# TensorE's order in the out product and the first MLP products, by a scheduler and written out

## The chip, the cores and the metric

The kernel runs on one core of a Trainium2 chip. The time is device microseconds (us) of one execution. Before the change three timed runs gave 2256.86, 2263.51 and 2263.76 us, median 2263.51.

## The reference

One layer of a decoder trunk, 1024 tokens of width 1024, float32: token mixing (dilated attention and an RWKV-7 branch, merged by gates), then an MLP. The stage at hand lies between the two halves:

```python
mix_out = merged @ w_out[l]
x = (x + gt1 * rms_norm(mix_out, norm_mix_post[l])).astype(x.dtype)

h = rms_norm(x, norm_ffn_pre[l]) * (1.0 + sc2) + sh2
f = jnp.square(jax.nn.relu(h @ w_ff1[l])) @ w_ff2[l]
```

## The kernel before

Each float32 operand is split into a high part (a cast on ScalarE) and a low part (a subtraction, mostly on VectorE), and each product is three matmuls: high by high, high by low, low by high. `split` (L64, L65) does this.

The out product (`out_product`) works by row blocks of 128 tokens, 0 to 7. `product(q, i, half)` is 24 matmuls (8 slices of the inner dimension by 3) for row block i and 512 of the 1024 columns. All first halves come first; each is copied from PSUM to `mx` (L993). A *row step* R then makes the second halves of one or two row blocks: two blocks use the two halves of one PSUM tile `d` (two buffers), each half a bank of its own. It copies them to `my` (L1014), sums squares on ScalarE (L1016), makes the factor of the first norm (`rr`, by `mean_rsqrt`, L1117 to L1127), multiplies (`junk`, L1025), adds to `x` on GpSimd and VectorE (L1027), sums squares again (L1030), makes the second factor and scales `x` on ScalarE (L1033).

A *transpose step* T takes the scaled `x` of a step: per row block two sets of four transposes into a PSUM tile `s` (two buffers, L1044). One set is read by two VectorE instructions (L1053, L1054), the other by four of ScalarE (L1049). Row blocks 0 to 3 give `hh0`, `hl0`, high and low part of the first 512 tokens of `h`; row blocks 4 to 7 give `h1`, and each of them a part of `T2`, one operand of the MLP's products (L1059 to L1061 and a split).

`ff1_head` makes products of the first 512 tokens by the left column halves of `w_ff1`, in pairs H of two groups, H0, H2, H4 and H6. A pair is four *quarters* of 12 matmuls, two in each half of one tile `d`: group 0 and group 1 with the upper half of the inner dimension (each copied to `u` on ScalarE, L1090), then both with the lower (each read by `ft`, L1100). Its weights come by DMA (`w_t`, three buffers) and are split to `w_h`, `w_l` (eight buffers each, one pair's worth).

`ff1` then makes the rest of the first MLP product by a seven-product scheme into tiles `m` (L1108, as the quarters). It begins with the operands `T3`, `T1`, `T4` and `B22`, made from `h1` and `hh0`, `hl0` of all 512 columns (L1146 to L1156 and splits; 20 instructions of VectorE over 1024 columns), and with sums and splits of weights (`t`, L1173 to L1176, `op`).

The order of each engine's instructions comes from a scheduler, which moves independent matmuls into each other's gaps; dependencies are by whole tile, so a write into one half of `d` waits for a read of the other half that stands ahead of it in the program. Instructions given to `keep_in_program_order` hold their order on their engine. The lines of the order in the program:

```python
todo.append((group, residual(group)))
if len(todo) > 1:
    transposed(*todo.pop(0))
```

so a transpose step is written one row step late, with H0 ahead of T7 and H2 to H6 behind it; where they stand in the end the scheduler decides.

Of the kernel before, what the change touches and what calls it, by code (L numbers as in the profile page):

```python
# [21 lines left out]
KT = D // 128  # L22
# [5 lines left out]
C_GATE = C_QKV + 3328  # L28
DFF = 4096
NH, NU, NF, NOP, NHW = 8, 4, 3, 12, 8  # L30
OGR = ((0, 1), (2, 3), (4,), (5,), (6,), (7,))
OPV = 0
OQ = 0
NBD, NFT, NLT, NW, NGT, NRK = 5, 6, 3, 4, 2, 4
# [15 lines left out]
class Block:  # L50
    def __init__(self, tc, ins, out, dbg=None):
        self.tc, self.nc, self.I, self.out, self.dbg = tc, tc.nc, ins, out, dbg or {}

    def dump(self, name, ap):
        if name in self.dbg:
            self.nc.sync.dma_start(self.dbg[name], ap)
# [908 lines left out]
    def out_product(self, cst, big, w1, ut, ft, psD, psS, xS):  # L965
        nc, tc = self.nc, self.tc
        hs = (slice(0, 512), slice(512, 1024))
        tc.keep_in_program_order(nc.scalar.preload_act_table_set("natural_log_exp_and_others"))
        with ExitStack() as es:
# [9 lines left out]
            def product(p, i, half):  # L979
                hi, lo = wos[half]  # L980
                mh, ml = self.mh[i // 4], self.ml_[i // 4]
                tl = slice(128 * (i % 4), 128 * (i % 4) + 128)
                for k in range(KT):
                    for n, (a, b) in enumerate(((mh, hi), (mh, lo), (ml, hi))):
                        nc.tensor.matmul(p, a[:, k, tl], b[:, k, :], start=k == 0 and n == 0,
                                         stop=k == KT - 1 and n == 2)

            for i in range(NT):
                if i % 2 == 0:
                    p = psD.tile([128, S], F32, name="d")  # L990
                q = p[:, hs[i % 2]]
                product(q, i, 0)
                nc.vector.tensor_copy(mx[:, i, :], q)  # L993
                junk = t2.tile([128, D], BF16, name="junk2", bufs=1)[:, 0:512]
                nc.scalar.activation(junk, mx[:, i, :], AF.Square, accum_out=ss[:, 0, i:i + 1])
            hhs, hls = [], []

            def residual(group):
# [8 lines left out]
                for n, i in enumerate(group):  # L1007
                    x = t2.tile([128, D], F32, name="x", bufs=4)
                    nc.sync.dma_start(x, self.w("x")[128 * i:128 * i + 128, :])
                    xs.append(x)  # L1010
                    q = p[:, hs[n]]
                    product(q, i, 1)
                    with tc.high_priority():
                        nc.vector.tensor_copy(my[:, n, :], q)  # L1014
                        junk = t2.tile([128, D], BF16, name="junk2", bufs=1)[:, 0:512]
                        nc.scalar.activation(junk, q if OQ else my[:, n, :], AF.Square, accum_out=ss[:, 1, i:i + 1])  # L1016
# [19 lines left out]
            def transposed(group, xs):  # L1036


                for n, i in enumerate(group):
                    x, tl = xs[n], slice(128 * (i % 4), 128 * (i % 4) + 128)  # L1040
                    for b in range(2):
                        pt = psS.tile([128, 4, 128], F32, name="s")
                        for k in range(4):
                            nc.tensor.transpose(pt[:, k, :], x[:, 512 * b + 128 * k:512 * b + 128 * k + 128],  # L1044
                                                self.ident)
                        ht = t2.tile([128, 4, 128], F32, name="ht") if i < 4 else self.h1[:, 4 * b:4 * b + 4, tl]
                        if b:
                            for k in range(4):
                                nc.scalar.activation(ht[:, k, :], pt[:, k, :], AF.Identity,  # L1049
                                                     scale=sc[:, 4 + k:5 + k], bias=sh[:, 4 + k:5 + k])  # L1050
                        else:
                            bc = lambda c: c[:, 0:4, None].to_broadcast([128, 4, 128])
                            nc.vector.tensor_tensor(ht, pt, bc(sc), OP.mult)  # L1053
                            nc.vector.tensor_tensor(ht, ht, bc(sh), OP.add)  # L1054
                        if i < 4:
                            self.split(ht, self.hh0[:, 4 * b:4 * b + 4, tl], self.hl0[:, 4 * b:4 * b + 4, tl])
                    if i >= 4:
                        t = t2.tile([128, 4, 128], F32, name="ht")
                        nc.vector.tensor_tensor(t, self.h1[:, 0:4, tl], self.hh0[:, 0:4, tl].bitcast(F32), OP.subtract)  # L1059
                        nc.vector.tensor_tensor(t, t, self.hl0[:, 0:4, tl].bitcast(F32), OP.subtract)  # L1060
                        nc.vector.tensor_tensor(t, self.h1[:, 4:8, tl], t, OP.subtract)  # L1061
                        self.split(t, self.T2[:, 0, :, tl], self.T2[:, 1, :, tl])

            todo = []
            for group in OGR:
                if group[0] == 0:
                    self.hh0, self.hl0 = [big.tile([128, KT, 512], F32R, name="big") for q in range(2)]
                if group[0] == 4:
                    self.h1 = big.tile([128, KT, 512], F32, name="big")
                    self.T2 = big.tile([128, 2, 4, 512], F32R, name="big")  # L1070
                todo.append((group, residual(group)))
                if len(todo) > 1:
                    transposed(*todo.pop(0))
            self.ff1_head(w1, ut, ft, psD, range(2))
            transposed(*todo[0])
            self.ff1_head(w1, ut, ft, psD, range(2, NH))

    def ff1_head(self, w1, ut, ft, psD, gs):

# [16 lines left out]
    def feature(self, ft, p, j, half):  # L1096
# [4 lines left out]
        nc.scalar.activation(t, t, AF.Square)  # L1101
        nc.sync.dma_start(self.fS[j // 4][:, j % 4, 512 * half:512 * half + 512], t)

    def quarter(self, p, a, b, start):

        for k, ((ah, al), (bh, bl)) in enumerate(zip(a, b)):
            for i, (s, m) in enumerate(((ah, bh), (ah, bl), (al, bh))):
                self.nc.tensor.matmul(p, s, m, start=start and k == 0 and i == 0, stop=k == len(a) - 1 and i == 2,  # L1108
                                      skip_group_check=not start)

    def mean_rsqrt(self, sm, v, pool=False):

# [299 lines left out]
```

## Time and profile before

| | |
|---|---|
| median of three timed runs | 2263.51 us |
| the profiled execution, and its span | 2252.45 us, 2250.7 us |
| TensorE / VectorE / ScalarE / GpSimd busy | 93 / 69 / 46 / 27% of the span |
| first matmul of `out_product` | 1472.9 us |
| first transposes of T01, T23, T7 | 1545.2, 1562.5, 1603.9 us |
| first matmul into `m` | 1640.04 us |

Times in rows are us from the start of the span. A row of a timeline is a run of like instructions with its start, its length, and in brackets the idle time of its engine ahead of it with what ended that. L numbers are lines of the kernel before. A busy TensorE is counted from modelled ends of pipelined matmuls: two matmuls that start 0.227 us apart each show 0.39 us.

### The profile page before, as it was taken

Reading aid. Unit: us, or ns where it says so; the run is one execution under the profiler, and the core shown is the slowest. Engines: PE = TensorE matmul, PEld = TensorE weight load, DVE = VectorE, ACT = ScalarE, POOL = GpSimd, SP = SyncE. Lnnn points to the kernel's source line nnn. Section 1 sums busy time; section 2 is a strip of 40 time slices with the busy share of each in tenths; the row PEclk is TensorE's granted clock in tenths of the full one; section 3 lists DMA queues with packets and bytes.
Section 4 is the critical chain, followed back from the end, with each engine's and each line's share of the span. In section 5 each row is a group of like instructions: output and inputs, shape, how many; then the busy total and the mean of one; then the engine's idle time right before and its main releaser. Section 6 shows DMA issues by size and latency. Waiting matters only on the chain. (4 is left out here: it accounts for less than half of the span.)

```text
span 2250.7 us, 28246 instructions
## 1 busy us (share of the span) xinstructions
PE 2083.3 (93%) x10002; PEld 1621.9 (72%) x10002; DVE 1559.3 (69%) x2857; ACT 1035.0 (46%) x2018; POOL 602.6 (27%) x455
## 2 busy tenths in 40 slices
PE   6899999988999989898989999999889999999997
PEld 2676766666777767676767778877667777788886
DVE  5845555458989787878777743436876553799988
ACT  4634533445454636454554442225744443533342
POOL 2504310321313131222122122201100000788850
PEclk9999999999999999999998999999999999999999
DMA  7513311110111110101011154432544333433232
GB/s 248 181 34 99 99 40 29 59 31 22 30 33 35 31 37 27 35 29 37 24 37 34 52 179 159 128 120 84 166 156 163 113 107 111 166 130 128 88 109 75
DMA packets 156315, 194.88 MB, mean 87 GB/s; under 512 B 10729, under 2 KB 110211, under 8 KB 154127
## 3 DMA queue, kind: packets, MB, share of 16 engines
q1 hardware_dynamic: 156175, 193.08, 25.8%
q8 instruction: 79, 1.29, 0.2%
q14 instruction: 61, 0.50, 0.1%
HBM read 152.14 MB, written 40.90 MB: 86 GB/s over the span
## 5 line engine op out<-in xcount | busy, mean ns | idle before, releaser
L307 PE MATMUL d<-hh,w_h 128*128 128x512 f32 x960 | 328.2, 414 | 8.0 <-ACT w_h L64 4.6
L307 PE MATMUL d<-hl,w_h 128*128 128x512 f32 x960 | 329.5, 413 | 2.9 <-DVE hl L280 2.9
L307 PE MATMUL d<-hh,w_l 128*128 128x512 f32 x960 | 324.2, 410 | 1.4 <-DVE w_l L65 1.3
L65 POOL TENSOR_TENSOR w_l<-w_t,w_h 128x256 fp32r<-128x256 f32 x160 | 128.3, 803 | 634.0 <-ACT w_h L64 288.7
L1108 PE MATMUL m<-op 128*128 128x512 f32 x1272 | 292.0, 391 | 6.3 <-DVE big L1344 2.4
L1108 PE MATMUL m<-big,op 128*128 128x512 f32 x1152 | 276.6, 401 | 8.0 <-ACT op L64 4.1
L1108 PEld LDWEIGHTS m<-op 128*128 128x128 f32 x1272 | 239.5, 189 | 58.5 <-POOL op L65 3.4
L1108 PEld LDWEIGHTS m<-big,op 128*128 128x128 f32 x1152 | 213.9, 189 | 70.8 <-DVE u L1219 5.3
L64 ACT CAST w_h<-w_t 128x256 fp32r<-128x256 f32 x272 | 108.4, 404 | 310.3 <-PE d L307 222.7
L307 PEld LDWEIGHTS d<-hh,w_h 128*128 128x128 f32 x960 | 180.4, 192 | 47.8 <-ACT w_h L64 5.8
L307 PEld LDWEIGHTS d<-hl,w_h 128*128 128x128 f32 x960 | 181.0, 192 | 44.9 <-issue 9.4
L307 PEld LDWEIGHTS d<-hh,w_l 128*128 128x128 f32 x960 | 180.1, 191 | 42.5 <-issue 7.9
L64 ACT CAST op<-t 128x512 fp32r<-128x512 f32 (+1 forms) x152 | 113.5, 775 | 174.5 <-PE m L1108 119.3
L153 POOL TENSOR_TENSOR macc<-macc,ada_t 128x512 f32<-128x512 f32 x56 | 87.2, 1559 | 179.5 <-ACT macc L151 160.7
L65 DVE TENSOR_TENSOR op<-t,op 128x512 fp32r<-128x512 f32 (+1 forms) x125 | 117.7, 962 | 20.5 <-ACT op L64 20.3
L1281 DVE TENSOR_TENSOR big<-big,m 128x1024 f32<-128x1024 f32 x88 | 104.7, 1210 | 11.9 <-PE m L1108 11.8
L1299 POOL TENSOR_TENSOR t<-big 128x1024 f32<-128x1024 f32 x7 | 23.1, 3303 | 325.8 <-DMA big<-in_w_ff_dram 325.4
L775 DVE TENSOR_TENSOR lt<-lt 64x30 f32<-64x30 f32 (+14 forms) x240 | 97.1, 404 | 8.2
L777 DVE TENSOR_TENSOR lt<-lt 64x30 f32<-64x30 f32 (+14 forms) x240 | 93.9, 391 | 7.7
L874 PEld LDWEIGHTS ch<-sv,fe 128*128 128x128 f32 x512 | 83.0, 190 | 20.2 <-DVE sv L877 8.9
L65 POOL TENSOR_TENSOR op<-t,op 128x1024 fp32r<-128x1024 f32 x27 | 88.4, 3275 | 7.1 <-ACT op L64 7.1
L65 DVE TENSOR_TENSOR w_l<-w_t,w_h 128x256 fp32r<-128x256 f32 x112 | 60.1, 545 | 40.3 <-ACT w_h L64 28.9
(381 smaller groups left out, 3888.4 us busy)
## 6 DMA issues: line engine op xcount, KB each, us to landing
w_t<-in_w_in_dram SPq DMA_DIRECT2D x240, 128.0 KB
ada_t<-in_ada_w_dram SPq DMA_DIRECT2D x64, 256.0 KB
fS<-ft SPq DMA_DIRECT2D x64, 256.0 KB
t<-in_w_ff_dram SPq DMA_DIRECT2D x16, 1024.0 KB
big<-fS SPq DMA_DIRECT2D x16, 1024.0 KB
big<-in_w_ff_dram SPq DMA_DIRECT2D x16, 1024.0 KB
x<-in_x_dram SPq DMA_DIRECT2D x16, 512.0 KB
ada_t<-in_ada_w_dram SPq DMA_DIRECT2D x16, 512.0 KB
```

The costliest lines, as they stand in the source:

```text
L64: nc.scalar.copy(hi, t)
L65: (eng or nc.vector).tensor_tensor(lo, t, hi.bitcast(F32), OP.subtract)
L153: nc.gpsimd.tensor_tensor(acc, acc, t, OP.add)
L307: nc.tensor.matmul(p[:, 512 * half + cs.start:512 * half + cs.stop], a, b[half][k][:, cs], start=k == ks[0] and i == 0, stop=k == ks[-1] a ...
L775: nc.vector.tensor_tensor(q, lb[:, s + 1:32, s:s + 1].to_broadcast([64, n, s]), lb[:, s:s + 1, 0:s].to_broadcast([64, n, s]), OP.mult)
L777: nc.vector.tensor_tensor(lb[:, s + 1:32, 0:s], lb[:, s + 1:32, 0:s], q, OP.add)
L874: nc.tensor.matmul(ps[h][:, c8, :], fe[b][:, h, c8, :], sv[h][b][:, c8, :], start=True, stop=True)
L1108: self.nc.tensor.matmul(p, s, m, start=start and k == 0 and i == 0, stop=k == len(a) - 1 and i == 2, skip_group_check=not start)
L1281: nc.vector.tensor_tensor(acc[nm][h], acc[nm][h], ps2[h], OP.add)
L1299: vb.tensor_tensor(t3, wr[:, k2, h2], wr[:, k1, h2], OP.subtract)
```

## The change

`OORDER` lists the steps R, T and H in words. The loop runs through them in that order, and every matmul and transpose of a step is kept in program order on TensorE. The first halves (ahead of the list) and the products into `m` (behind it) stay with the scheduler. `product`, `transposed` and `quarter` pass their instruction through `pin`.

```diff
-OGR = ((0, 1), (2, 3), (4,), (5,), (6,), (7,))
+OORDER = "R01 R23 T01 R4 R5 T23 R6 T4 H0 R7 T5 H2 T6 H4 T7 H6"
...
-                        nc.tensor.matmul(p, a[:, k, tl], b[:, k, :], start=k == 0 and n == 0,
-                                         stop=k == KT - 1 and n == 2)
+                        self.pin(nc.tensor.matmul(p, a[:, k, tl], b[:, k, :], start=k == 0 and n == 0,
+                                                  stop=k == KT - 1 and n == 2))
...
-            todo = []
-            for group in OGR:
-                if group[0] == 0:
+            self.pinned = True
+            xs = {}
+            for step in OORDER.split():
+                kind, rows = step[0], tuple(int(r) for r in step[1:])
+                if kind == "H":
+                    self.ff1_head(w1, ut, ft, psD, range(rows[0], rows[0] + 2))
+                    continue
+                if step == "R01":
                     self.hh0, self.hl0 = [big.tile([128, KT, 512], F32R, name="big") for q in range(2)]
-                if group[0] == 4:
+                if step == "R4":
...
-                todo.append((group, residual(group)))
-                if len(todo) > 1:
-                    transposed(*todo.pop(0))
-            self.ff1_head(w1, ut, ft, psD, range(2))
-            transposed(*todo[0])
-            self.ff1_head(w1, ut, ft, psD, range(2, NH))
+                if kind == "R":
+                    xs[rows] = residual(rows)
+                else:
+                    transposed(rows, xs.pop(rows))
+            self.pinned = False
...
+    def pin(self, ins):
+        return self.tc.keep_in_program_order(ins) if self.pinned else ins
```

TensorE at T23 before. `d_12763` is the tile of R6; `s_12637` and `s_12647` are the two sets of row block 2, `s_12659` the first of row block 3.

```order
L985 MATMUL d_12763<-wol_12088,big_11282 128x512
L1044 MATMUL s_12637<-ident_149,x_12432 128x128 x4
L1044 MATMUL s_12647<-ident_149,x_12432 128x128 x4
L985 MATMUL d_12763<-wo_12087,big_11284 128x512
L985 MATMUL d_12763<-wo_12087,big_11282 128x512
L985 MATMUL d_12763<-wol_12088,big_11282 128x512
...
L1044 MATMUL s_12659<-ident_149,x_12461 128x128 x4
```

The same place now; `d_12637` is the tile of R5, `d_12741` that of R6.

```order
L986 MATMUL d_12637<-wo_12087,big_11284 128x512
L1045 MATMUL s_12697<-ident_149,x_12432 128x128 x4
L1045 MATMUL s_12707<-ident_149,x_12432 128x128 x4
L1045 MATMUL s_12719<-ident_149,x_12461 128x128 x4
L1045 MATMUL s_12729<-ident_149,x_12461 128x128 x4
L986 MATMUL d_12741<-wo_12087,big_11282 128x512
```

The four sets of T23 stand together, and R6 has moved behind them.

TensorE at T7 before. `d_13060` is the tile of H2, `d_13171` that of H4; `s_13038` and `s_13045` are the sets of row block 7.

```order
L1108 MATMUL d_13060<-big_12327,w_l_13082 128x512
L1108 MATMUL d_13171<-big_12327,w_h_13174 128x512
L1108 MATMUL d_13171<-big_12328,w_h_13174 128x512
L1108 MATMUL d_13171<-big_12327,w_l_13175 128x512
L1108 MATMUL d_13060<-big_12327,w_h_13087 128x512
...
L1044 MATMUL s_13038<-ident_149,x_12847 128x128 x4
L1044 MATMUL s_13045<-ident_149,x_12847 128x128 x4
L1108 MATMUL d_13060<-big_12327,w_h_13099 128x512
```

T7 now; `d_13149` is the tile of H4, `d_13282` that of H6.

```order
L1116 MATMUL d_13149<-big_12328,w_h_13194 128x512
L1116 MATMUL d_13149<-big_12327,w_l_13195 128x512
L1045 MATMUL s_13260<-ident_149,x_12936 128x128 x4
L1045 MATMUL s_13267<-ident_149,x_12936 128x128 x4
L1116 MATMUL d_13282<-big_12327,w_h_13285 128x512
```

T7 has moved from the third quarter of H2 to the end of H4, and matmuls of two pairs no longer mix.

VectorE behind T7 before: `big<-s` is the first reader of its transposes, `t_13418`, `t_13422` and `t_13426` lead to the operands of `ff1`, `w_l` are splits of weights of the pairs.

```order
L1053 TENSOR_TENSOR big<-s,m_590 128x4x128
L65 TENSOR_TENSOR w_l<-w_t,w_h 128x256
L1054 TENSOR_TENSOR big<-big,m_590 128x4x128
L1059 TENSOR_TENSOR ht<-big 128x512
...
L1146 TENSOR_TENSOR t_13418<-big 128x1024
L65 TENSOR_TENSOR w_l<-w_t,w_h 128x256 x2
L1146 TENSOR_TENSOR t_13422<-big 128x1024
L65 TENSOR_TENSOR big<-t_13418,big 128x1024
L65 TENSOR_TENSOR big<-big 128x1024
```

The same place now.

```order
L66 TENSOR_TENSOR w_l<-w_t,w_h 128x256 x6
L1054 TENSOR_TENSOR big<-s,m_590 128x4x128
L1055 TENSOR_TENSOR big<-big,m_590 128x4x128
L1060 TENSOR_TENSOR ht<-big 128x512
...
L1154 TENSOR_TENSOR t_13418<-big 128x1024
L1154 TENSOR_TENSOR t_13422<-big 128x1024
L66 TENSOR_TENSOR big<-t_13418,big 128x1024
L1159 TENSOR_TENSOR t_13426<-big 128x1024
```

All splits `w_l` now stand ahead of T7's readers; behind them the operands of `ff1` follow each other directly.

## Rows read from the trace of the kernel before

**Rows 1.** The chain that ended last, 1440 to 1800 us, by line.

```profile
by line: PE m L1108 33.4%; DMA t<-in_w_ff_dram 5.0%; PE d L1108 4.7%; issue 3.3%; DVE big L65 2.6%; DVE junk L1025 2.2%; DVE x L1027 1.6%; DVE op L65 1.5%; DMA w_t<-in_w_ff_dram 1.4%; POOL x L1027 1.2%; ACT big L64 1.2%; ACT junk L1030 1.0%
```

**Rows 2.** Busy time of each engine by stages of the span.

```profile
core 0: us, PE busy (x) PEld busy (x) DVE busy (x) ACT busy (x) POOL busy (x), PEclk, DMA share, GB/s
1530.00:1603.90 73.90, 63.38 (x290) 49.22 (x289) 57.16 (x130) 49.53 (x120) 14.80 (x8) 0.98 0.35 125
1603.90:1641.20 37.30, 27.25 (x117) 20.27 (x115) 34.37 (x45) 24.94 (x46) 0.00 (x0) 1.00 0.45 144
1641.20:1910.00 268.80, 266.89 (x1114) 206.94 (x1114) 152.20 (x235) 121.38 (x208) 0.00 (x0) 0.99 0.39 130
```

**Rows 3.** What TensorE waited for, 1465 to 1720 us: total, times, longest.

```profile
PE d L1108 <- ACT u L1090: 6.8, 5, 3.0
```

**Rows 4.** Timeline of TensorE, 1465 to 1516 us, at the halves of `d`.

```profile
1481.16 32.44 PE L985 MATMUL d<-big 128*128 128x512 f32 x139 [1.54 <-DVE mx L993]
...
1506.64 6.96 PE L985 MATMUL d<-big 128*128 128x512 f32 x30
1513.44 0.39 PE L985 MATMUL d<-wo,big 128*128 128x512 f32 x1
...
1514.39 5.74 PE L985 MATMUL d<-big 128*128 128x512 f32 x24
```

**Rows 5.** Timeline of VectorE, 1531 to 1541 us: row blocks 0 to 2.

```profile
1531.22 0.69 DVE L1014 COPY my<-d 128x512 f32<-128x512 f32 x1 [5.83 <-PE d L985]
...
1539.44 0.74 DVE L1025 SCALAR_TENSOR_TENSOR junk<-my,rr,g 128x512 f32<-128x512 f32 x1
```

**Rows 6.** Timeline of TensorE: transposes of T01, T23 and T7.

```profile
1545.18 1.06 PE L1044 MATMUL s<-ident,x 128*128 128x128 f32 x8 [0.99 <-ACT x L1033]
...
1549.22 0.60 PE L1044 MATMUL s<-ident,x 128*128 128x128 f32 x4
...
1562.47 1.06 PE L1044 MATMUL s<-ident,x 128*128 128x128 f32 x8 [1.75 <-issue]
...
1568.60 0.60 PE L1044 MATMUL s<-ident,x 128*128 128x128 f32 x4
...
1603.87 1.04 PE L1044 MATMUL s<-ident,x 128*128 128x128 f32 x8
```

**Rows 7.** Timeline of TensorE: a quarter of H0, three quarters of H6, first `m`.

```profile
1578.39 0.72 PE L1108 MATMUL d<-big,w_h 128*128 128x512 f32 x2 [1.31 <-ACT u L1090]
...
1625.44 0.72 PE L1108 MATMUL d<-big,w_h 128*128 128x512 f32 x2 [2.98 <-ACT u L1090]
...
1629.14 0.73 PE L1108 MATMUL d<-big,w_h 128*128 128x512 f32 x2 [0.68 <-ACT u L1090]
...
1632.87 0.73 PE L1108 MATMUL d<-big,w_h 128*128 128x512 f32 x2 [0.69 <-ACT ft L1100]
...
1640.04 0.73 PE L1108 MATMUL m<-big,op 128*128 128x512 f32 x2 [4.13 <-ACT op L64]
1641.20 4.14 PE L1108 MATMUL m<-big,op 128*128 128x512 f32 x10 [0.42 <-DVE op L65]
```

**Rows 8.** Timeline of VectorE behind T7.

```profile
1616.86 2.35 DVE L1151 TENSOR_TENSOR t<-big 128x1024 f32<-128x1024 f32 x2
1620.17 0.42 DVE L65 TENSOR_TENSOR w_l<-w_t,w_h 128x256 fp32r<-128x256 f32 x1 [0.97 <-ACT w_h L64]
1621.00 0.76 DVE L65 TENSOR_TENSOR w_l<-w_t,w_h 128x256 fp32r<-128x256 f32 x2 [0.41 <-ACT w_h L64]
```

**Rows 9.** Busy time of the instructions on `w_l` behind T7 (TensorE, its loads, VectorE, GpSimd).

```profile
1603.90:1641.20 37.30, 13.67 (x36) 6.57 (x35) 5.11 (x13) 0.00 (x0) 1.00 0.45 144
```

**Rows 10.** Granted clock 1600 to 1610 us, and TensorE behind the stop of 2.32 us.

```profile
1600.00:1610.00 10.00, 9.76 (x40) 7.62 (x38) 5.91 (x14) 7.07 (x16) 0.00 (x0) 0.83 0.42 128
...
1599.16 0.50 PE L1108 MATMUL d<-big,w_l 128*128 128x512 f32 x1 [2.32 <-DVE w_l L65]
1600.21 1.03 PE L1108 MATMUL d<-big,w_h 128*128 128x512 f32 x2
```

More of the change, by code (lines that the diff above doesn't have):

```diff
@@ L1043, in transposed @@
                         for k in range(4):
-                            nc.tensor.transpose(pt[:, k, :], x[:, 512 * b + 128 * k:512 * b + 128 * k + 128],
-                                                self.ident)
+                            self.pin(nc.tensor.transpose(pt[:, k, :], x[:, 512 * b + 128 * k:512 * b + 128 * k + 128],
+                                                         self.ident))
                         ht = t2.tile([128, 4, 128], F32, name="ht") if i < 4 else self.h1[:, 4 * b:4 * b + 4, tl]
@@ L1062, in transposed @@
                         self.split(t, self.T2[:, 0, :, tl], self.T2[:, 1, :, tl])
-            todo = []
-            for group in OGR:
-                if group[0] == 0:
+            self.pinned = True
[6 more added lines that the diff above has]
+                if step == "R01":
                     self.hh0, self.hl0 = [big.tile([128, KT, 512], F32R, name="big") for q in range(2)]
-                if group[0] == 4:
+                if step == "R4":
                     self.h1 = big.tile([128, KT, 512], F32, name="big")
                     self.T2 = big.tile([128, 2, 4, 512], F32R, name="big")
-                todo.append((group, residual(group)))
-                if len(todo) > 1:
-                    transposed(*todo.pop(0))
-            self.ff1_head(w1, ut, ft, psD, range(2))
-            transposed(*todo[0])
-            self.ff1_head(w1, ut, ft, psD, range(2, NH))
+                if kind == "R":
+                    xs[rows] = residual(rows)
+                else:
+                    transposed(rows, xs.pop(rows))
+            self.pinned = False
     def ff1_head(self, w1, ut, ft, psD, gs):
@@ L1107, in quarter @@
             for i, (s, m) in enumerate(((ah, bh), (ah, bl), (al, bh))):
-                self.nc.tensor.matmul(p, s, m, start=start and k == 0 and i == 0, stop=k == len(a) - 1 and i == 2,
-                                      skip_group_check=not start)
+                self.pin(self.nc.tensor.matmul(p, s, m, start=start and k == 0 and i == 0, stop=k == len(a) - 1 and i == 2,
+                                               skip_group_check=not start))
     def mean_rsqrt(self, sm, v, pool=False):
```

## Prediction

> **What bounds the kernel now.** I read the chain that ended last first: from 1641 us on it is nearly all TensorE (matmuls into `m`), but from 1534 to 1641 us it is made of short pieces of VectorE and ScalarE [rows 1]. The table by stages says the same from the other side [rows 2]: TensorE is busy 63.4 of 73.9 us and then 27.3 of 37.3 us in the stage that the change touches, and 266.9 of 268.8 us behind it. So any shift of the first matmul into `m` (now 1640.04 us, without a break from 1641.20 us) goes to the end one to one; nothing behind it has room to give it back. The list of waits of TensorE names its stops here [rows 3]: ScalarE's reads of `d` (`u`, 6.8 us), and the single longest, 4.13 us, stands ahead of the first `m` [rows 7]. That one counts. After the last transposes (row block 7, T7, at 1603.87 us) VectorE must finish the operands of the MLP's first half, and it is busy 34.4 of those 37.3 us [rows 2]. The moment of T7 therefore sets the end: T7 plus VectorE's list, then the `m` products.
>
> **The change part by part.** No instruction is added or removed; GpSimd's order is the same, VectorE, ScalarE and the queue of SyncE follow TensorE's new order. I walk TensorE in its new order and on the clock of the trace of before. Its pace is 0.227 us a matmul (30 in 6.80 us, 1506.64 to 1513.44) [rows 4], so 24 of a product are 5.44 us and 12 of a quarter 2.72 us.
>
> 1. *Two halves of one `d` no longer have anything between them.* Both halves are one tile, and the second half's first matmul waits for the copy of the first half. Before, four matmuls of the next tile fill that gap, 1513.44 to 1514.39 us, 0.95 us [rows 4]. After, row block 7 still starts at 1514.39 but with those four undone; 48 matmuls later, at 1525.3, R0 waits its 0.95; R1 and R2 end at 1537.1. R2's copy now stands on VectorE behind the fourth `junk`, which ended at 1540.18 before [rows 5]; its chain starts 0.5 us later (row 1's copy at 1531.7 against 1531.22), the copy no longer stands ahead of it, so it ends near 1540.8 and R3 runs 1540.9 to 1546.3. TensorE stands 3.7 us, where before it did 20 matmuls of R4.
>
> 2. *T01.* Row 0's `x` is ready at about 1545.7 (1545.18 before), so the first set goes at 1546.3. There are two `s` buffers: the third and fourth set wait for the readers of the first two. Before, the fourth came 4.04 us behind the first (1545.18, 1549.22) [rows 6] with matmuls of R4 between them; now nothing is between. End with 0.4 us of transposes: 1550.7.
>
> 3. *R4, R5*: 48 matmuls, to 1561.6. *T23*: before, its first set came 13.25 us behind T01's fourth (1549.22 to 1562.47) and the fourth set 6.13 us behind the first [rows 6]. After: 1550.3 + 13.25 = 1563.6, end 1563.6 + 6.13 + 0.4 = 1570.1. TensorE comes at 1561.6, so 8.5 us go for 16 transposes; before, R6 and most of R7 ran in these gaps.
>
> 4. *R6* 5.44 us, to 1575.6; *T4*: 8 transposes show 1.04 us [rows 6], of which 0.2 lie beside the next matmul, so 0.8; its second set waits for a reader of T23's fourth, an estimate of 0.6 us more: 1.4, to 1577.0. H0 started at 1573.45 before, with R7 already done.
>
> 5. *The pairs H.* Within a pair each of the quarters 2, 3 and 4 waits for ScalarE's read of the quarter before, again because both halves are one tile. Where a pair ran undisturbed (the last one), its quarters started 3.70 and 3.73 us apart [rows 7]: 2.72 of matmuls and 0.99 of wait. In the new order nothing may stand in these gaps, so a pair is 3 x 3.715 + 2.72 = 13.9 us. H0 to 1590.9, R7 (5.44) to 1596.3, T5 (0.8) to 1597.1, H2 to 1611.0, T6 to 1611.8, H4 to 1625.7. **T7 starts at 1625.7 us; before at 1603.87.** The reason is plain from the order: before, one quarter of H2 and all of H4 and H6 stood behind T7, now H6 alone.
>
> 6. *From T7 to the first `m`.* Before 37.3 us (1603.87 to 1641.20). VectorE's order behind T7 holds the same operands, 20 instructions over 1024 columns that read all row blocks of `h1` (1.13 us apart, two in 2.35 us [rows 8]), then the first sums and splits of weights. What leaves it are the 13 splits `w_l` that stood among them [rows 9], 0.34 us apart [rows 8], 4.4 us, and the two waits of 0.97 and 0.41 us for `w_h` [rows 8]: 31.5 us remain. The unbroken `m` start is then 1625.7 + 31.5 = 1657.2 us against 1641.20: **+16.0 us**. H6 ends at 1625.7 + 0.8 + 13.9 = 1640.4, so TensorE will stand about 17 us, although before that it has fewer waits for weights: the `w_l` of H6 are now all ahead of T7 and hidden under H2 and H4.
>
> 7. *The clock.* After a stop of 2.32 us (to 1599.16) TensorE ran at 1.2 GHz for a few us: two matmuls took 1.03 us, where at pace they show 0.227 + 0.39 = 0.62, and the stretch shows 0.83 granted [rows 10]. After the 4.13 us stop ahead of `m` ten matmuls took 4.14 us [rows 7], 1.9 us more than at pace. The trace has no dense run behind a stop of 17 us here; I bound its extra cost by nothing (the same dip, already paid) and by 3.8 us (twice the 1.9 us), and take 1, nearer to the stop whose row lies next to it.
>
> Sum: +16.0 + 1 = **+17 us**. The profiled execution took 2252.45 us (span 2250.7); with the change 2269.5. The three timed runs have a median of 2263.51, 11.1 us above the profiled one, and I put the change on the median: **2280.5 us**.
>
> Bounds of the parts that the trace does not show: the wait in a pair between 0.68 us of idle time (the smallest [rows 7], nine of them instead of 0.99: -2.8 us) and 1.6 us where ScalarE has casts ahead of the read (1.31 us of idle time at 1578.39 [rows 7] and the 0.3 us a restart: +5.5 us); T01 and T23 between their bare transposes (3.3 us of the 12.9 us above: -9.6 us) and 3 us more; T7 to `m` between 29 and 34 us (34.4 of 37.3 us are busy [rows 2], so with all idle time and the 4.4 us gone 30.0 remain; 1 us for faster starts, 2.5 us for waits on ScalarE). All lower ends together leave +2 us, all upper ends +27.5 us.
>
> **The rivals.** *A: the gaps inside a pair close.* The Trainium skill, Perfetto Trace Analysis, section Matmuls, says that matmul groups which rotate through PSUM banks overlap one group's evacuation with the next group's matmuls; the halves of `d` are two banks, so by that rule quarter 2 need not wait for quarter 1's copy. What speaks against it here are the rows: 3.70 us from quarter to quarter, each stop ended by `u` or `ft` of ScalarE [rows 7]; the wait is one the program asks for, by tile. If the stops went all the same, nine before T7 would: T7 at 1625.7 - 9 x 0.99 = 1616.8 us, `m` at 1648.3, +7 us: 2270.6 us.
>
> *B: not slower.* TensorE's stops go and T7 is early enough. The point is T7 at 1641.20 - 31.5 = 1609.7 us. Ahead of T7 stand 144 + 192 + 192 = 528 matmuls of the out product and three pairs from 1472.9 us on (119.7 us) and 56 transposes (5.8 us): with no stop at all T7 is at 1598.4, `m` at 1629.9, -11 us: 2252.5 us. For it: today VectorE is idle 16.7 of the 73.9 us from 1530 to 1604 us [rows 2]. Against it: the two kinds of stop by tile alone (2 x 0.95, 9 x 0.99) and the 1.54 us at 1481.16 [rows 4] bring it to 1610.7, past the point, before any wait of T01 and T23.
>
> *C: no change.* VectorE and ScalarE are what bounds 1530 to 1641 us whatever TensorE's order is, since the chain runs through them [rows 1]; their work is the same, so `m` starts at 1641: 2263.5 us. Against it: T7 is no longer limited by the row chain (row 7's `x` is asked for 29 us after R7's end), so VectorE will stand idle before T7 and its list cannot start early.
>
> *D: worse.* ScalarE's order puts casts, squares and row scales ahead of `u` and `ft` in H0 and H2; with 1.6 us instead of 0.99 a wait (+5.5) and T23 3 us later it is +25.5 us: 2289 us.
>
> **How the numbers follow.** A measurement of this kernel can tell about 0.3% (6.8 us) from no change. Forecast (+10 to +22 us) 0.66, D 0.12, A 0.10, C 0.07 with small shifts to either side, B 0.05. Slower by over 0.3%: the forecast, D and 0.07 of A, which lies just past that bound: 0.85; within: C and the rest of A: 0.10; faster: B, 0.05. The range leaves out B, C and the far half of D: 2269 to 2289 us; the forecast's own is 2273.5 to 2285.5.
>
> **What would show it.** In the profile after: T7 between 1620 and 1630 us; 15 to 18 us of idle time of TensorE between the last `d` matmul of a pair and the `m` products, ended by VectorE's `op` or ScalarE's casts; quarters of a pair about 3.7 us apart; a stop of 3 to 4 us ahead of R3 on the copy of row 2; over 6 us lost in T23; VectorE without `w_l` behind T7; the stretch behind the first `m` unchanged in length (268.8 us, [rows 2]). Wrong would make it: T7 ahead of 1610 us, or an `m` start that does not follow T7 by 29 to 34 us.

## The result, and the profile after

The changed kernel takes 2279.48 us (median of seven runs, 2271.56 to 2287.03) against 2262.92 us of the kernel before beside it (seven runs). The two medians are 16.6 us apart; the ratio estimated from the runs is 1.0086, with a 95% interval of [1.0064, 1.0108], or +14.5 to +24.4 us, so the change is slower beyond the noise. The forecast was 2280.5 us and slower. The execution that was profiled took 2279.48 us, with a span of 2277.8 us.

The two traces are not aligned in time: the first matmul of `out_product` stands at 1472.89 us before and at 1479.27 us after, though the code ahead of it is the same (the last section returns to this). Everything below is therefore counted from that matmul, called the **start**: its moment is taken off a row's time, and a time of the prediction (given on the time axis of before) has 6.4 us added to be compared with a row of after.

| us from the start | before | forecast | after |
|---|---|---|---|
| first transposes of T01 | 72.3 | 73.4 | 76.1 |
| T23 | 89.6 | 90.7 | 93.9 |
| T4 | 98.7 | 102.7 | 107.5 |
| T7 | 131.0 | 152.8 | 158.6 |
| first `m`; unbroken `m` | 167.1; 168.3 | -; 184.3 | 187.0; 190.4 |
| end of the span | 777.8 | 794.8 | 798.5 |

So the stage is 20.7 us longer in these two executions: +27.6 at T7, -5.5 from T7 to the unbroken `m` (37.3 to 31.8 us), -1.4 behind it (609.5 to 608.1 us). The unbroken `m` is where the last chain of work enters its first run of matmuls into `m`: the row below for after, 1641.20 us [rows 7] before.

```profile
1669.66 7.12 PE m L1116 x20
```

That is the fifth matmul into `m`, behind a stop of 0.12 us; before it was the third. Counted from the third in both (168.3 and 189.05 us), the way from T7 is 6.9 us shorter (37.3 to 30.5 us) and the way from there to the end is 609.5 us in both. So the last -1.4 us is no gain: it is two matmuls more that are already done. Where the expectations below name 31.8 us, they count to the fifth.

The same stages as in [rows 2], of after; the second is from T7 to the unbroken `m`, the third as long as that of before. Columns: length of the stretch, then busy time of each engine, then granted clock, DMA.

```profile
core 0: us, PE busy (x) PEld busy (x) DVE busy (x) ACT busy (x) POOL busy (x), PEclk, DMA share, GB/s
1536.40:1637.90 101.50, 81.13 (x355) 63.33 (x354) 61.82 (x142) 59.63 (x141) 13.98 (x8) 0.95 0.35 118
1637.90:1669.70 31.80, 15.27 (x62) 10.46 (x60) 30.48 (x33) 17.65 (x27) 0.00 (x0) 0.81 0.25 82
1669.70:1938.50 268.80, 266.67 (x1110) 206.96 (x1111) 151.94 (x235) 120.62 (x206) 0.00 (x0) 0.99 0.39 129
```

VectorE was the engine that worked through the second stage before (34.4 of 37.3 us) and still is (30.5 of 31.8 us); TensorE's share there fell from 27.3 to 15.3 us. The third stage did not move: 266.7 us busy of 268.8, before 266.9. Ahead of T7 VectorE and TensorE now have about 40 and 20 us idle in 101.5: neither of them bounds that stretch by its work, the engines wait for each other.

What TensorE waited for, 1465 to 1730 us of after: total, times, longest (answers to [rows 3]).

```profile
PE m L1116 <- ACT op L65: 14.0, 2, 13.1
PE d L1116 <- ACT u L1095: 7.3, 8, 1.6
PE d L986 <- DVE my L1015: 4.9, 2, 4.1
PE s L1045 <- ACT ht L1050: 3.5, 2, 2.0
```

TensorE's timeline of after: ahead of R3, a further row of R3, T01, T23, T4, T5, T6, H4's second and third quarters, T7, first `m` (answers to [rows 4, 6, 7, 10]).

```profile
1548.19 0.80 PE L986 MATMUL d<-wo,big 128*128 128x512 f32 x1 [4.11 <-DVE my L1015]
...
1549.21 1.05 PE L986 MATMUL d<-wo,big 128*128 128x512 f32 x2
...
1555.34 1.03 PE L1045 MATMUL s<-ident,x 128*128 128x128 f32 x8
...
1559.13 0.66 PE L1045 MATMUL s<-ident,x 128*128 128x128 f32 x4 [1.53 <-ACT ht L1050]
...
1573.18 1.07 PE L1045 MATMUL s<-ident,x 128*128 128x128 f32 x8 [2.48 <-ACT x L1034]
1576.25 1.09 PE L1045 MATMUL s<-ident,x 128*128 128x128 f32 x4 [2.00 <-DVE ht L1054]
1579.32 1.11 PE L1045 MATMUL s<-ident,x 128*128 128x128 f32 x4 [1.99 <-ACT ht L1050]
1586.73 1.03 PE L1045 MATMUL s<-ident,x 128*128 128x128 f32 x8
...
1607.21 1.03 PE L1045 MATMUL s<-ident,x 128*128 128x128 f32 x8
...
1622.06 1.04 PE L1045 MATMUL s<-ident,x 128*128 128x128 f32 x8
...
1627.45 0.73 PE L1116 MATMUL d<-big,w_h 128*128 128x512 f32 x2 [1.59 <-ACT u L1095]
...
1631.22 0.73 PE L1116 MATMUL d<-big,w_h 128*128 128x512 f32 x2 [0.76 <-ACT u L1095]
...
1637.85 1.03 PE L1045 MATMUL s<-ident,x 128*128 128x128 f32 x8
...
1666.24 1.22 PE L1116 MATMUL m<-big,op 128*128 128x512 f32 x2 [13.13 <-ACT op L65]
1668.32 8.46 PE L1116 MATMUL m<-big,op 128*128 128x512 f32 x22 [0.86 <-ACT op L65]
```

Read from the top: most written-out gaps are stops in brackets that [rows 4 and 6] did not have, since a neighbour's matmuls filled them (ahead of T23 there was one of 1.75 us already). Two matmuls of R3 take 1.05 us instead of 0.62: they ran at 1.2 GHz behind the 4.11 us stop. The granted clock (the third column from the right) in R3, and in T23 and R6:

```profile
1550.00:1555.00 5.00, 5.00 (x20) 4.06 (x19) 0.66 (x4) 3.21 (x6) 0.00 (x0) 0.84 0.18 73
...
1575.00:1580.00 5.00, 1.76 (x7) 1.40 (x8) 3.88 (x13) 4.31 (x13) 0.00 (x0) 0.55 0.60 210
1580.00:1585.00 5.00, 5.00 (x20) 4.03 (x19) 4.49 (x9) 3.69 (x8) 2.79 (x1) 0.77 0.36 108
```

T5 to T6 and T6 to T7 are one pair each: 14.85 and 15.79 us.

VectorE behind T7, of after (answers to [rows 8]): operands with no `w_l` between them, then sums of weights (L1181 to L1184).

```profile
1643.56 2.35 DVE L1154 TENSOR_TENSOR t<-big 128x1024 f32<-128x1024 f32 x2
...
1649.49 1.22 DVE L1160 TENSOR_TENSOR t<-t,big 128x1024 f32<-128x1024 f32 x1
1650.62 1.22 DVE L1159 TENSOR_TENSOR t<-big 128x1024 f32<-128x1024 f32 x1
...
1664.85 0.68 DVE L1182 TENSOR_TENSOR t<-t,t 128x512 f32<-128x512 f32 x1
```

The operands come 1.13 us apart, as before; the sum at 1664.85 is what ScalarE's `op` at 1665.56 and with it the first `m` waited for.

### The profile page after: what moved, and what is told of

Its sections match the earlier page's. It is cut to its first block, busy times and chain, and to the rows that moved or that the text cites. A ratio compares the mean times of both kernels' runs of the same rounds, so it can differ in the third digit from the quotient of the medians.

```text
span 2277.8 us, 28258 instructions
## 1 busy us (share of the span) xinstructions
PE 2092.6 (92%) x10002; PEld 1629.7 (72%) x10002; DVE 1556.7 (68%) x2857; ACT 1037.3 (46%) x2018; POOL 602.5 (26%) x455
## 5 line engine op out<-in xcount | busy, mean ns | idle before, releaser
L66 DVE TENSOR_TENSOR op<-t,op 128x512 fp32r<-128x512 f32 (+1 forms) x125 | 117.8, 961 | 20.7 <-ACT op L65 20.5
L1289 DVE TENSOR_TENSOR big<-big,m 128x1024 f32<-128x1024 f32 x88 | 104.8, 1211 | 11.8 <-PE m L1116 11.6
```

Source lines behind the costliest of these rows:

```text
L66: (eng or nc.vector).tensor_tensor(lo, t, hi.bitcast(F32), OP.subtract)
L1289: nc.vector.tensor_tensor(acc[nm][h], acc[nm][h], ps2[h], OP.add)
```

## The experiments

Positions are us from the start, each from the one profile of that run. The ratio is to the kernel before on the same chip (its median 2256.4 to 2257.7 us there; 2262.92 us in the row of the changed kernel).

| run | T7 | first `m` | end | end against before | ratio [95%] |
|---|---|---|---|---|---|
| before | 131.0 | 167.1 | 777.8 | | |
| changed | 158.6 | 187.0 | 798.5 | +20.7 | 1.0086 [1.0064, 1.0108] |
| e12 changed, again | 157.7 | 186.1 | 799.0 | +21.2 | 1.0095 [1.0072, 1.0118] |
| e1 pairs behind | 132.3 | 178.1 | 785.3 | +7.5 | 1.0029 [1.0010, 1.0047] |
| e2 own tiles | 148.5 | 180.8 | 791.7 | +13.9 | 1.0063 [1.0042, 1.0083] |
| e3 unpinned | 128.2 | 170.1 | 785.6 | +7.8 | 1.0027 [1.0009, 1.0046] |
| e4 fifth pair | 158.1 | 189.4 | 792.0 | +14.2 | 1.0059 [1.0036, 1.0081] |
| e5 weights first | 158.6 | 175.4 | 798.6 | +20.8 | 1.0078 [1.0051, 1.0106] |
| e6 before, weights first | 131.0 | 163.5 | 781.3 | +3.5 | 1.0008 [0.9986, 1.0029] |
| e7 three edits | 130.0 | 166.7 | 777.7 | -0.1 | 0.9999 [0.9980, 1.0018] |
| e8 four `s` | 159.8 | 188.1 | 801.6 | +23.8 | 1.0098 [1.0069, 1.0126] |
| e9 before, own tiles | 130.3 | 155.9 | 774.9 | -2.9 | 0.9987 [0.9971, 1.0002] |
| e10 rows between | 131.2 | 169.1 | 781.4 | +3.6 | 1.0001 [0.9984, 1.0018] |
| e11 filled stand | 159.1 | 187.5 | 802.2 | +24.4 | 1.0096 [1.0076, 1.0117] |

Two cautions. The intervals of e2 and e4 overlap that of the changed kernel, so their gains rest on the positions. And the end of one profile is not exact: e6 and e10 end 3.5 and 3.6 us later than before with ratios of 1.0008 and 1.0001, so differences of the end under some 4 us are not read as effects here.

### Pairs behind the transposes (e1)

```diff
-OORDER = "R01 R23 T01 R4 R5 T23 R6 T4 H0 R7 T5 H2 T6 H4 T7 H6"
+OORDER = "R01 R23 T01 R4 R5 T23 R6 T4 R7 T5 H0 T6 T7 H2 H4 H6"
```

> The list becomes R01 R23 T01 R4 R5 T23 R6 T4 R7 T5 H0 T6 T7 H2 H4 H6: R7 ahead of H0 and T7 behind it, everything still pinned, so the stops in T01, T23 and inside the pairs stay as they are. Theory 1 (T7's place sets the end: VectorE's list of 31.5 us cannot start earlier): T7 moves some 25 us forward, three pairs (41.7 us) stand behind it, the m products start when TensorE is done with H6, about 12 us earlier than in the changed kernel: 2267.5 us (2262 to 2272), idle time ahead of m under 4 us. Rival (the stops of the pinned order cost the time, wherever T7 stands): the sum of the stops is the same, 2279 us, m follows H6 at the same place.

TensorE of e1: T7's last set, a quarter, the first `m`.

```profile
1607.11 0.66 PE L1045 MATMUL s<-ident,x 128*128 128x128 f32 x4 [0.79 <-DVE big L1054]
...
1629.44 0.73 PE L1116 MATMUL d<-big,w_h 128*128 128x512 f32 x2 [0.68 <-ACT u L1095]
...
1651.54 6.12 PE L1116 MATMUL m<-big,op 128*128 128x512 f32 x24 [1.19 <-ACT op L65]
```

Two thirds of the loss are back (13.2 of 20.7 us), as the theory said: the place of T7 ahead of the pairs is the main cause. But the first `m` is 45.8 us behind T7 (178.1 less 132.3), not 28 to 32, and the stand ahead of `m` is 1.19 us instead of 13.1: now TensorE itself is late, with three pairs of 13.8 to 14.7 us, stops and all, between T6 and the first `m`. T7 is where the kernel before has it, and the kernel is still 0.3% slower.

### Each half of a pair in its own tile (e2)

```diff
-            d = psD.tile([128, S], F32, name="d")
-            pair = [(g, d[:, 512 * (g - g0):512 * (g - g0) + 512]) for g in (g0, g0 + 1)]
+            pair = [(g, psE.tile([128, 512], F32, name="e")) for g in (g0, g0 + 1)]
```

> The changed order, but the two halves of a pair H are two tiles of 512 columns with two buffers in banks that were free, instead of two halves of one tile. Theory (the stops in a pair are a dependency by whole tile): quarters start 2.72 us apart instead of 3.70, nine stops of 0.99 us ahead of T7 go, T7 and the m products come 9 us earlier: 2270.5 us (2267 to 2275), idle time ahead of m unchanged (13 to 15 us). Rival (ScalarE's reads and matmuls cannot overlap, whatever the tile): quarters stay 3.7 us apart, 2279.5 us. Second rival (T7's lateness comes from the row chain, not from the pairs): quarters 2.72 us apart, but T5 to T7 stand and m starts as before, 2279 us.

TensorE of e2: T5, T6, T7, the first `m`.

```profile
1605.29 1.03 PE L1045 MATMUL s<-ident,x 128*128 128x128 f32 x8
...
1617.09 1.03 PE L1045 MATMUL s<-ident,x 128*128 128x128 f32 x8
...
1628.89 1.03 PE L1045 MATMUL s<-ident,x 128*128 128x128 f32 x8
...
1661.17 8.15 PE L1115 MATMUL m<-big,op 128*128 128x512 f32 x24 [20.32 <-ACT op L65]
```

The pairs run without a stop, 11.80 us from T to T instead of 14.85 and 15.79, and T7 is 10.1 us earlier. The first `m` follows T7 by 32.3 us, with TensorE standing still for 20.3 of them: VectorE's list behind T7 sets `m`. The expectation had the stand at 13 to 15 us and so the whole gain at `m`; the gain at the end is 6.8 us, less than at T7. Part of the rest is that VectorE first reads T7's transposes 2.34 us behind their start, at 1631.23 (0.75 us in the changed kernel, at 1638.60), behind splits `w_l` that wait for ScalarE.

### The order of the program without the pins (e3)

```diff
-            self.pinned = True
+            self.pinned = False
```

> The list of steps stays as the program's order, but nothing is kept in program order: the scheduler may fill gaps again (it puts T7 between quarters of H2 and mixes matmuls of R6, R7, H0 into T23). Theory (the loss comes from what pinning does: no filling and T7 behind H4): about the kernel before, 2263 us (2259 to 2267). Rival (the order of the steps itself, H0 ahead of R7 and transposes late, costs): 2275 us or more.

The scheduler moves T7 back to 128.2 us, and 12.9 of the 20.7 us are back. A remainder of 0.3% stays that belongs to the order of the program, not to the pins. The theory's 16 us were too many; the result lies between it and the rival.

### A fifth pair in the stand (e4)

```diff
-NH, NU, NF, NOP, NHW = 8, 4, 3, 12, 8
+NH, NU, NF, NOP, NHW = 10, 4, 3, 12, 8
-OORDER = "R01 R23 T01 R4 R5 T23 R6 T4 H0 R7 T5 H2 T6 H4 T7 H6"
+OORDER = "R01 R23 T01 R4 R5 T23 R6 T4 H0 R7 T5 H2 T6 H4 T7 H6 H8"
```

> The changed order with one more pair, H8, behind H6 (ten instead of eight groups made in the pairs; their 48 matmuls leave the m products, 10.9 us). Theory (behind H6 TensorE stands 13 to 14 us for VectorE's list alone): H8 with its stops takes 13.9 us of that stand, the m products begin within 3 us of where they begin in the changed kernel and are 10.9 us shorter: 2270 us (2267 to 2274). Rival (TensorE's work ahead of m is what counts, or the eight more splits of weights lengthen VectorE's list as much): 2279 us or more.

The first `m` of e4:

```profile
1670.04 0.73 PE L1116 MATMUL m<-big,op 128*128 128x512 f32 x2 [1.86 <-ACT op L65]
```

It waits 1.86 us instead of 13.13 and comes 2.4 us later; from it to the end are 602.6 us instead of 611.5, since 48 matmuls (10.9 us) are already done. Net 6.5 us: the stand is real idle time that useful work can fill.

### Weights of group 0 first (e5, e6)

```diff
+        nxt = weights(0)
         for q in range(2):      # operands T3, T1, T4, B22
...
-        nxt = weights(0)
```

> The changed kernel with one edit in `ff1`: group 0's weight sums and splits stand in the program ahead of the operands T3, T1, T4 and B22 instead of behind them; TensorE's written order stays. Theory (what bounds the start of the products into `m` is VectorE's and ScalarE's list behind T7, of which the weights' `op` splits are the last part, and nothing of that list could be brought ahead of T7 in the changed kernel because VectorE had no work there that was written early enough): T7 stays at 158 us from the first matmul of the out product, the unbroken products into `m` start 22 to 26 us behind T7 instead of 31.8, TensorE's stand ahead of them is 3 to 8 us instead of 13, and the time falls by 6 to 12 us against the changed kernel (about 2268 to 2274 where the kernel before has 2263). Rival (the list behind T7 has only the T operands' chain as its bound, the weights are done anyway when it ends): start of `m` and time within 2 us of the changed kernel's. Second rival: the earlier sums delay VectorE's reads for the pairs and transposes and T7 comes 4 us or more later, so that the time doesn't fall.

> The kernel before (the scheduler's order on TensorE) with the same one edit: group 0's weight sums and splits ahead of the operands T3, T1, T4, B22. In the kernel before TensorE has pairs to do during that list and stands still only 4 us ahead of `m`, so theory: at most 4 us earlier, ratio to the kernel before 0.998 to 1.000. Rival: the sums displace reads on VectorE that release T4 to T7 or the pairs, and it is slower by 2 to 6 us, ratio 1.001 to 1.003.

TensorE of e5: the first runs of matmuls into `m`.

```profile
1653.26 0.74 PE L1116 MATMUL m<-big,op 128*128 128x512 f32 x2 [1.54 <-ACT op L65]
1654.30 5.39 PE L1116 MATMUL m<-big,op 128*128 128x512 f32 x22 [0.30 <-ACT op L65]
1670.27 1.22 PE L1116 MATMUL m<-big,op 128*128 128x512 f32 x2 [10.58 <-ACT op L65]
```

VectorE of e5: the same sum of weights (L1162), twice.

```profile
1649.30 0.69 DVE L1162 TENSOR_TENSOR t<-t,t 128x512 f32<-128x512 f32 x1
...
1668.88 0.68 DVE L1162 TENSOR_TENSOR t<-t,t 128x512 f32<-128x512 f32 x1
```

Two products into `m` (24 matmuls) start 11.6 us earlier, and the rest waits: the next one needs an `op` whose sum VectorE makes at 1668.88, behind all operands (the second appearance of the line, so I take it for group 1's). The stand was moved and hardly shortened: its four stops (1.54, 0.30, 10.58 and then 0.86 us) make 13.3 us, against 14.1 in the changed kernel. The time is the changed kernel's, as the first rival said, though the start of `m` is not. In the kernel before (e6) no gain can be told either; its interval holds both theory and rival.

### All three (e7)

```diff
+OORDER = "R01 R23 T01 R4 R5 T23 R6 T4 R7 T5 H0 T6 T7 H2 H4 H6"
+            pair = [(g, psE.tile([128, 512], F32, name="e")) for g in (g0, g0 + 1)]
+        nxt = weights(0)   # ahead of the operands
```

> Three edits on the changed kernel together: the list has the pairs behind the transposes (T4 R7 T5 H0 T6 T7 H2 H4 H6), each half of a pair has its own PSUM tile, and group 0's weight sums and splits stand ahead of the operands T3, T1, T4 and B22. By the theory each of the three takes another part: T7 at 132 us from the first matmul of the out product as in the run with T7 early, the three pairs behind it 10.5 us each instead of 13.9, and the list behind T7 22 to 26 us instead of 31.8. Together `m` starts unbroken at 160 to 168 us from the first matmul of the out product (the kernel before 168.3, the run with T7 early 178.1) and the time is 0 to 8 us under the kernel before: ratio 0.9965 to 1.000. Rival (the two dips of the clock that all written orders pay in T01 and T23 and the reads by VectorE keep it late): `m` at 172 to 178 us, ratio 1.0015 to 1.003.

TensorE of e7: T7 and the first `m`.

```profile
1599.57 2.07 PE L1045 MATMUL s<-ident,x 128*128 128x128 f32 x8 [3.60 <-ACT x L1034]
...
1636.23 0.72 PE L1115 MATMUL m<-big,op 128*128 128x512 f32 x2 [1.19 <-ACT op L65]
1638.78 5.41 PE L1115 MATMUL m<-big,op 128*128 128x512 f32 x22 [1.83 <-DVE op L66]
```

The written order reaches the kernel before, and no more; the unbroken `m` starts at 169.2 us, past the 160 to 168 expected. By the positions, e1's 13.2 us and e2's 6.8 us make 20.0 of the 20.8 us recovered here, and the third edit alone (e5) gave nothing: the place of the pairs and the stops inside them account for the loss, if their effects add. That they add is argued, not shown: no run had those two edits without the third.

### Four tiles `s` (e8)

```diff
-                psS = self.pool(ep, "psS", 2, space=PSUM)
+                psS = self.pool(ep, "psS", 4, space=PSUM)
```

> The changed kernel with four PSUM tiles `s` instead of two: a transpose set waits for the readers of the set four ahead of it, not two. Theory (the stops inside T01 and T23 are waits for `s`, 0.6 + 1.5 us and 2.5 + 2.0 + 2.0 us in the changed kernel, and with them go the half-clock stretches behind them): T7 at 152 to 154 us from the first matmul of the out product instead of 158.6, `m` the same 31.8 us behind it, the time 5 to 7 us under the changed kernel's. Rival (TensorE then runs ahead of VectorE and ScalarE, which are the bound there, and waits as long at the next read, of `d` by `my` or of `u`): T7 and time within 2 us of the changed kernel's.

TensorE of e8: T23 and T4.

```profile
1563.76 3.64 PE L1045 MATMUL s<-ident,x 128*128 128x128 f32 x16 [4.72 <-ACT x L1034]
1576.99 1.94 PE L1045 MATMUL s<-ident,x 128*128 128x128 f32 x8 [3.06 <-ACT x L1034]
```

The stops for `s` are gone (16 transposes in one run), and TensorE stands instead for `x`, 4.72 and 3.06 us, which ScalarE and VectorE bring no more than 0.8 us earlier. The rival is right: in T23 and T4 the other engines set the pace, and T7 is at 159.8 us. That pace belongs to the written order, though: the scheduler's order feeds them earlier, and the kernel before has T4 at 98.7 us where e8 has it at 106.7.

### Before with own tiles (e9) and rows between (e10)

e9 is the kernel before with the edits of e2 and e5; e10 is e7 with the transposes taken by row block:

```diff
+OORDER = "R01 R23 T0 R4 T1 R5 T2 R6 T3 T4 R7 T5 H0 T6 T7 H2 H4 H6"
```

> The kernel before (TensorE's order left to the scheduler) with each half of a pair in its own PSUM tile and group 0's weight sums first in `ff1`. Theory (the pairs' stops are the only thing in the kernel before that own tiles can take, and the scheduler has filled most of them already): the stops for `u` and `ft` between T4 and `m`, 2.98 + 0.68 + 0.69 us and their like, go; `m` starts unbroken 162 to 168 us from the first matmul of the out product instead of 168.3; ratio to the kernel before 0.997 to 1.000. Rival (the list of VectorE and ScalarE behind T7, 31.8 us in the changed kernel, sets `m` and starts no earlier): no change, ratio 0.9995 to 1.001.

> The kernel with three edits (pairs behind the transposes, own tiles, weights first) and the transposes of row blocks 0 to 3 taken apart: T0 R4 T1 R5 T2 R6 T3 T4 R7 T5 H0 T6 T7 H2 H4 H6, so that the products of a row step stand between two transpose steps instead of stops. Theory (the stops in T01 and T23, 2.1 + 6.5 us, and the half-clock stretches that follow them in all written orders are TensorE's alone): T7 at 118 to 126 us from the first matmul of the out product instead of 130, `m` at 158 to 165 instead of 169, and the time 4 to 10 us under the kernel before, ratio 0.9955 to 0.998. Rival (VectorE and ScalarE, which make `x` of each row step and read each `s`, already set the pace there, as with four tiles `s`): the stops move to the waits for `x`, T7 within 3 us of 130 and ratio 0.999 to 1.001.

T7 of e10:

```profile
1614.86 1.94 PE L1045 MATMUL s<-ident,x 128*128 128x128 f32 x8 [4.18 <-ACT x L1034]
```

e9 has the lowest ratio of all, and its interval, [0.9971, 1.0002], still holds no change. Its first two products into `m` start 11 us earlier, but the third waits 4.86 us, until 168.9 us, where 162 to 168 was expected. e10 meets the same wall as e8: T7 is at 131.2 us, behind a 4.18 us wait for `x`, and ratio 1.0001 is the rival's.

### Dummy matmuls in the stand (e11), and the changed kernel again (e12)

```diff
+            d = psD.tile([128, S], F32, name="d")
+            for n in range(4):
+                self.quarter(d[:, 0:512], ...)   # hh0, hl0 by themselves; nobody reads d
             self.pinned = False
```

> The changed kernel with 48 matmuls (four quarters of `hh0` and `hl0`, into a PSUM tile that nobody reads) behind H6, so that TensorE is busy for 10.9 of the 13 us in which it stands ahead of `m`. Theory (the stand costs, beyond its length, the half clock that follows it: 22 matmuls of `m` in 8.46 us instead of 5.39 and about 9 us at the half clock in all): the first 22 matmuls of `m` at 5.4 us, no half-clock stretch at `m`, and the time 3 to 5 us under the changed kernel's. Rival (the first products into `m` wait for VectorE's `u` and ScalarE's `op` in any case, so that a slower TensorE is hidden there): the clock stays up but the time is within 1.5 us of the changed kernel's.

> The changed kernel itself once more, beside the others on this chip, so that their differences to it can be read without a second chip: ratio to the kernel before 1.0086, between 1.0064 and 1.0108. Any theory expects this; a ratio outside it would mean that differences under 0.3 per cent between the chips can't be read.

TensorE of e11 from the dummies on.

```profile
1655.23 11.04 PE L1120 MATMUL d<-big 128*128 128x512 f32 x48
1668.49 0.74 PE L1120 MATMUL m<-big,op 128*128 128x512 f32 x2 [2.22 <-ACT op L65]
1670.58 8.41 PE L1120 MATMUL m<-big,op 128*128 128x512 f32 x22 [1.35 <-ACT op L65]
```

The same 22 matmuls in e12, the changed kernel again.

```profile
1656.59 7.24 PE L1116 MATMUL m<-big,op 128*128 128x512 f32 x22 [0.86 <-ACT op L65]
```

TensorE's busy time in e11 (the columns are length, busy, granted clock, DMA share, GB/s) during the dummies, across the stops and behind them.

```profile
1655.20:1666.30 11.10, 11.07 (x49) 1.00 0.06 24
1666.30:1670.50 4.20, 0.74 (x2) 0.92 0.00 0
1670.50:1679.50 9.00, 8.29 (x22) 0.66 0.38 117
```

Both expectations failed on the clock: TensorE was busy for 11 us at 2.4 GHz, then came two short stops, and the next 22 matmuls into `m` again ran mostly at 1.2 GHz, in 8.41 us as against 8.46 and, in e12, 7.24. By the runs the time is e12's. So making the stand short did not spare the half clock, and no price of its length beyond that can be seen in the time. e12 lies inside the interval of the first comparison, so the other runs may be read against it.

## Why the prediction came out right

The chain of the argument held: TensorE's order puts T7 late, VectorE's list behind T7 keeps its length less the `w_l` splits, and behind `m` nothing gives time back. The term that was sized wrong is T7's: +21.8 us forecast, +27.6 measured.

- **T7 to `m`** (step 6): 31.5 us forecast; measured 30.5 to the third matmul into `m`, which the forecast counted to, and 31.8 to the fifth; 32.3 to the first `m` in e2 with T7 moved by 10 us. It holds only while pairs do not fill TensorE behind T7 (e1: 45.8 us).
- **Pairs** (step 5): forecast 14.7 us with the transposes, measured 14.85 from T5 to T6 and 15.79 from T6 to T7, where H4's second quarter stood idle 1.59 us for `u`. Counted as the forecast counts a wait (4.60 us from quarter to quarter, less 2.72) that is 1.88 us, past the upper bound of 1.6.
- **T23** (step 3): fourth set 6.13 us behind the first forecast, 6.14 measured (1573.18 to 1579.32). The stop ahead of R3 (step 1): 3.7 forecast, 4.11 measured.
- **T7 itself** was 5.8 us later than forecast. By the differences of the table and of the rows: 2.7 us are lost by T01 (the copy for R3 0.9 us late, then R3 at 1.2 GHz for a part, its 24 matmuls in 7.15 us from 1548.19 to T01, instead of 5.44); 0.5 more by T23; 1.6 from T23 to T4, at 1.2 GHz for a part (four transposes of T23 show 1.11 us instead of 0.60 [rows 6], and R6 follows them with 0.77 granted); 1.1 in H4; in H0 and H2 forecast and trace agree within 0.2 us.
- **The clock** (step 7) was put in the wrong place. I gave it 1 us at `m`. There the 22 matmuls from the third on take 8.46 us instead of 6.94, and nothing of it is left at the end: 609.5 us from the third matmul in both (610.8 in e12). What it took was ahead of T7, behind the stops of R3 and T23, which steps 1 and 3 counted as waits only.

The sum was +17 us, the profiles give +20.7 and the runs +19.5: the mechanism was right and the term of T7 (+21.8) too small by 5.8 us, of which about 3 us are the clock's (an estimate: 1.7 in R3 and most of the 1.6 from T23 to T4) and 2 are late reads of `d` (0.9 ahead of R3, 1.1 in H4). The other two terms erred the other way: T7 to `m` gave back 6.9 us instead of 5.8, and the 1 us at `m` was not there.

That 2280.5 us stands 1 us from the median measured is luck. The seven runs lie 15.5 us apart, and the sum of +17 us stands against +16.6 by the medians, +19.5 by the ratio and +20.7 by the profiles. Of the signs named, three were just missed: T7 at 1631.5 us on the axis of before (1620 to 1630), the stop ahead of R3 of 4.11 us (3 to 4), and 14.1 us of idle time ahead of `m` (15 to 18).

Three slips in the working changed nothing. The upper ends add up to +28.0 us, not +27.5. The ten matmuls of step 7, counted like the two beside them (9 x 0.227 + 0.39 = 2.43 us), cost 1.7 us more than at pace, not 1.9. And the chain from 1641 to 1800 us is not nearly all TensorE: it is 75.6% matmuls into `m` and 11.3% DMA of weights. The shift went through to the end all the same.

**The rivals.** A (stops in pairs go) did not happen: the quarters of after still start 3.69 to 4.60 us apart (3.77 from 1627.45 to 1631.22). What it would have given is e2: it priced 8.9 us of T7, e2 measures 10.1 there, of which 6.8 reach the end. The Trainium skill's rule (Perfetto Trace Analysis, section Matmuls), that groups rotating through PSUM banks overlap evacuation with matmuls, holds in e2, where each bank is a tile of its own (11.80 us for a pair and its transposes), and not where two banks are one tile (14.85 and 15.79 us). B needed T7 at 136.8 us from the start or earlier; e1 has it at 132.3 and is slower than before all the same, so T7 early is not enough: the pairs' stops then stand on TensorE's way to `m`. C fell with T7 (VectorE idle 39.7 of 101.5 us ahead of it), though its ground holds in part: in e7, e8 and e10 TensorE stood 3.06 to 4.72 us for ScalarE's `x` at T23, T4 or T7, and no written order got past that. The scheduler's did: T23 at 89.6 us and T4 at 98.7 before, 93.5 and 106.7 in e8. D's long wait came once, 1.88 us in H4, and not in all nine.

What stays open: why e3, with the scheduler free again, keeps 0.3%. Its T7 is early, its `m` runs from 170.1 us with a second stop of 2.84 us at 1661.05, and no run took those apart. Open, too, is what the third edit gives in e7.

## What to carry to other kernels

Before an order is written out, look in the trace for what the scheduler had put into each wait: in this kernel a wait by tile cost little as long as a neighbour's work stood in it, and all of it once the neighbour was pinned elsewhere. Place the producer of the longest list on another engine (here T7, the last input of VectorE's operands) ahead of work that can wait, and keep that other work (three pairs) behind it as cover. Two dependent halves of one tile are worth splitting into two tiles only once what ends next is known: own tiles took 10 us at T7 and 7 at the end in the written order, and in the scheduler's order, together with the weights first (e9), could not be told from nothing.

## What the runs showed of the chip

The start of the stage, behind the same lines of the program in all fourteen profiled executions, lay anywhere between 1468.44 us (e12) and 1483.67 us (e10): 15 us, nearly the size of the effect. The same kernel profiled twice (the changed one) starts at 1479.27 and 1468.44 and has spans of 2277.8 and 2267.4, but 798.5 and 799.0 us from the start to the end. In this pair every position of the table repeats within 1 us when counted from the start of the stage, while the spans differ by 10. Why the start moves is not shown.

In e11 TensorE did 11 us of matmuls at 2.4 GHz, stood 2.22 and 1.35 us with two matmuls between, and then worked through 9 us with a mean granted clock of 0.66: by those rows an estimated 6 us at 1.2 GHz with matmuls running ((1 - 0.66) x 9 / 0.5). In e7 stops of 1.19 and 1.83 us at the same place, again with two matmuls between, were followed by 22 matmuls in 5.41 us; in e10 stops of 1.19 and 1.34 us by 22 in 6.93:

```profile
1654.84 6.93 PE L1115 MATMUL m<-big,op 128*128 128x512 f32 x22 [1.34 <-DVE op L66]
```

So the length of such stops does not tell by itself whether the clock falls behind them; what does is not shown here.
